# First attention of a decoder trunk: each head's product with V in its own half of the array's columns, one output bank, three transposition banks

## Chip, cores and metric

The kernel runs on one core of one Trainium2 chip. The metric is the device time of one execution in microseconds, the median of several runs. The engines are TensorE (PE; its weight loads are listed as PEld), VectorE (DVE), ScalarE (ACT), GpSimd (POOL) and SyncE (SP), which issues the DMAs. Each engine works through its own instructions in order and waits on semaphores of the others.

## The reference

The reference is one step of a two-layer decoder for a prompt of 1024 tokens and 64 sample tokens, width 1024. Layer one is a sparse attention with 16 heads of 64 and 2 KV heads; layer two is differential attention; each is followed by an MLP with a squared ReLU. The change touches only the prompt part of layer one. There each head has three branches, whose outputs are added with gates:

```
s = jnp.einsum('btkgd,bckd->bkgtc', qg, kc);  p_cmp = softmax(where(c_ok, s, NEG));  o_cmp = p_cmp @ vc
... the same over the selected blocks -> o_sel (with 16 blocks of 64 in all, every earlier block is selected)
... the same over the last 512 positions -> o_win
out = o_cmp * g[..., 0:1] + o_sel * g[..., 1:2] + o_win * g[..., 2:3]
```

## The kernel before

`nsa_prompt` works on 64 units, one for each pair of heads (p, 8 of them) and block of 128 query rows (i, taken in the order 0, 7, 1, 6, 2, 5, 3, 4). A unit has two halves.

`scores` does, for each head s of the pair, the score products on PE into PSUM tiles S (two tiles of two banks each), the row maxima on DVE (L692), the exponentials on ACT into an SBUF tile P (L695; six P tiles, so three units), a reciprocal on DVE (L699) and, on POOL, the scaling of P's three parts by gate and sum (L702). An S tile is free again when ACT has read it.

`values` takes the scaled P of both heads. It has nb = 3 to 14 blocks of 128 keys (branch 0 has one, branch 1 has i + 1, branch 2 up to five). PE transposes every block of P into a PSUM bank `tr`, two blocks of two heads to a bank (L110), and DVE or ACT, by turns, copies the bank to SBUF as PT (L99 or L97). There are two `tr` banks. Then the products with V follow, 64 columns of V as weights and PT as the moving operand, into a bank `av` (two of them). Before the change, one matmul has both heads side by side (256 columns), and the blocks go by turns to the upper and the lower 64 partitions of `av`, so that two matmuls, in the two halves of the array's columns, stand next to each other; with an odd number of blocks the last one is done head by head. The two halves are then added: ACT copies the first half to `oh` (L746), and DVE adds the second half to it, once for each head (L748), into the output tile oT.

All matmuls with V and all transpositions have f32 operands. A matmul with V is two records in the trace, a transposition one.

The generators `prep`, `scores` and `values` are interleaved by `stagger`: a tuple (start, length, steps, generator) spreads the steps over units of time, and a scheduler then puts the instructions into an order for each engine by when it expects operands and buffers to be there. The order is fixed when the program is built. The first matmuls of `values` are kept behind its last transposition (`issue_after`).

Of the kernel before, what the change touches and what calls it, by code (L numbers as in the profile page):

```python
# [12 lines left out]
AF = mybir.ActivationFunctionType  # L13
OP = mybir.AluOpType
AX = mybir.AxisListType
PSUM = bass.MemoryType.PSUM
# [46 lines left out]
def stagger(gens):  # L63

    order = [(t + (i + 0.5) * d / n, k) for k, (t, d, n, _) in enumerate(gens) for i in range(n)]
    for _, k in sorted(order):
        next(gens[k][3], None)
    for g in gens:
        run(g[3])


class Step:
# [551 lines left out]
    def nsa_prompt(self, oT):  # L624
        nc, io = self.nc, self.io
        cmN, A, B, V = self.cmN, self.A, self.B, self.V
        with ExitStack() as ctx:

            qp = self.pool(ctx, bufs=2, side="right")
            sp = self.pool(ctx)  # L630
            Sp, trp, avp = (self.pool(ctx, bufs=2, space=PSUM) for _ in range(3))
            st = {}

            def prep(p):
                k = p // 4
                X = [(sp if p % 2 else qp)("X", [128, NP], F32R, bufs=2) for _ in range(2)]
                st[p] = X
                qn = qp("qn", [128, 8, 128])
                nc.sync.dma_start(qn, self.zq[0:NP, p * 128:p * 128 + 128].rearrange("(t p) c -> p t c", p=128))
                for g in range(2):  # L640
                    cs = slice(g * 512, g * 512 + 512)
                    ps = trp("tr", [128, 512]) if p else Sp("S", [128, 1024])[:, 0:512]
                    for i in range(4):
                        self.tr(ps[:, i * 128:i * 128 + 128], qn[:, 4 * g + i, :], 128)
                    for s in range(2):
                        self.qk_prep(ps, s * 64, X[s][k * 64:k * 64 + 64, cs], X[s][64 - k * 64:128 - k * 64, cs])
                        yield
# [59 lines left out]
            def scores(p, i):  # L707
                for s in range(2):
                    yield from score(p, i, s)

            def values(p, i):


                k = p // 4
                ks = slice(k * 64, k * 64 + 64)
                P, w1, j0 = zip(*(st[p, i, s] for s in range(2)))
                w1, j0 = w1[0], j0[0]

                blocks = [(0, V[0][:, ks])]
                blocks += [(64 + j * 128, V[1][:, j, ks]) for j in range(i + 1)]  # L720
                blocks += [(64 + w1 + (j - j0) * 128, V[2][:, j, ks]) for j in range(j0, i + 1)]
                nb = len(blocks)
                PT = sp("PT", [128, 14, 2, 128], bufs=2)
                for x0, x1 in [(max(x, 0), x + 2) for x in range(-(nb % 2), nb, 2)]:
                    ps = trp("tr", [128, 2, 2, 128])
                    for x in range(x0, x1):
                        for s in range(2):
                            o = blocks[x][0]
                            last = self.tr(ps[:, x - x0, s], P[s][:, o:o + 128], 128)
                    self.n_p += 1  # L730
                    self.hi("va"[self.n_p % 2], PT[:, x0:x1], ps[:, 0:x1 - x0])
                    yield
                av = avp("av", [128, 256])
                todo = [(x, None) for x in range(nb - 1, nb % 2 - 1, -1)] + [(0, s) for s in range(2) if nb % 2]
                with self.tc.issue_after(last.ins):
                    for c, (x, s) in enumerate(todo):
                        h = slice(c % 2 * 64, c % 2 * 64 + 64)
                        y = PT[:, x] if s is None else PT[:, x, s]
                        if s is None:
                            o, y = av[h], y.rearrange("p a b -> p (a b)")  # L740
                        else:
                            o = av[h, s * 128:s * 128 + 128]
                        self.mm(o, blocks[x][1], y, c < 2, c >= len(todo) - 2)
                yield
                oh = sp("oh", [64, 256], bufs=2)
                nc.scalar.activation(oh, av[0:64], AF.Copy)  # L746
                for s in range(2):
                    nc.vector.tensor_tensor(oT[p][s * 64:s * 64 + 64, i * 128:i * 128 + 128],  # L748
                                            av[64:128, s * 128:s * 128 + 128], oh[:, s * 128:s * 128 + 128], OP.add)

            units = [(p, i) for p in range(8) for i in (0, 7, 1, 6, 2, 5, 3, 4)]
            gens = [(-1, 1, 4, prep(0))] + [(8 * p + 0.5, 7, 4, prep(p + 1)) for p in range(7)]
            for u, (p, i) in enumerate(units):
                ng = (i + 1 + min(i + 1, 5) + 2) // 2
                gens.append((u, 1, 4 if i < 3 else 8, scores(p, i)))
                gens.append((u + 1.2, 1, ng + 1, values(p, i)))
            stagger(gens)


# [811 lines left out]
```

## Time and profile before

| what | value |
|---|---|
| median of 3 runs | 3484.68 us (3480.68 to 3485.0) |
| the profiled execution | 3483.36 us |
| its span, first to last instruction | 3481.6 us (1.76 us lie around it) |
| first attention (first to last product with V) | about 480 to 995 us |
| PE busy over the span | 3351.3 us (96%) |
| DVE, ACT, POOL busy over the span | 1930.0, 1224.7, 749.1 us |

Busy time is the time in which an engine has an instruction recorded. The recorded end of a matmul is modelled, so a PE that is shown as busy may still stand still for a moment. A wait is idle time of an engine and is put down to the instruction that released it.

### The profile page before, as it was taken

The page shows a single profiled execution, that of the slowest core. Times are in us where ns is not written, and L with a number is a line of the kernel's source. Part 1 is how long each engine was busy: PE and PEld are TensorE (multiplying, and loading weights), DVE is VectorE, ACT ScalarE, POOL GpSimd, SP SyncE. Part 2 cuts the span into 40 slices and gives each one's busy share as a digit, 9 for nine tenths or more (in the row PEclk, how much of TensorE's full clock was granted, in tenths as well). Part 3 has the DMA queues.
Part 4 walks back from the last instruction along what each step waited for, and adds up shares of the span by engine and source line. Part 5 has one row for each costly group of instructions (what it writes and reads, how often), then busy time and mean ns, then how long its engine had stood idle before and what let it go on. Part 6 is the DMA issues. An engine that isn't in the chain of part 4 may idle for free.

```text
span 3481.6 us, 57136 instructions
## 1 busy us (share of the span) xinstructions
PE 3351.3 (96%) x21902; PEld 2821.0 (81%) x21902; DVE 1930.0 (55%) x4110; ACT 1224.7 (35%) x2976; POOL 749.1 (22%) x1036
## 2 busy tenths in 40 slices
PE   8989889999999999999999998999989999999998
PEld 7879666666679999999998876677769999999998
DVE  5355666666665544454447213777775444444445
ACT  5122466666653111111114121677763211111111
POOL 1242234444420001110004203222230100011102
PEclk9999999999999999999999999999999999999999
DMA  7333410000022111111113223666632111111111
GB/s 249 123 115 96 139 41 7 7 13 1 1 70 73 39 41 49 49 48 44 37 43 132 93 76 98 205 219 224 200 101 65 57 43 37 43 49 49 45 36 52
DMA packets 238283, 270.87 MB, mean 78 GB/s; under 512 B 19802, under 2 KB 186874, under 8 KB 237946
## 3 DMA queue, kind: packets, MB, share of 16 engines
q1 hardware_dynamic: 238010, 267.23, 24.2%
q8 instruction: 172, 2.82, 0.3%
q14 instruction: 101, 0.83, 0.1%
HBM read 229.81 MB, written 41.50 MB: 78 GB/s over the span
## 4 chain that ended last, share of the span: by engine, by line
PE 82%; DVE 6%; ACT 4%; SPq 2%; DMA 2%; issue 2%; POOL 1%; DVEq 0%; ACTq 0%; POOLq 0%
PE dn L107 26%; PE up L107 22%; PE ps L107 11%; PE S L107 6%; PE av L107 6%; PE tr L110 6%; PE hid L107 2%; ACT P L695 2%; SPq L143 2%; PE tr L107 1%; DVE ml L692 1%; POOL P L702 1%; DMA out_dram<-in_state_nsa_win_dram 1%; DVE PT L99 1%; DMA kv<-in_cache_nsa_sel_dram 0%
## 5 line engine op out<-in xcount | busy, mean ns | idle before, releaser
L1078 DVE TENSOR_TENSOR xT<-xT,dn 128x512 f32<-128x512 f32 (+2 forms) x768 | 404.3, 530 | 497.2 <-PE dn L107 496.3
L107 PE MATMUL dn<-xh,dh 128*128 128x512 f32 (+2 forms) x1536 | 504.5, 328 | 0.7 <-DVE xT L1078 0.7
L107 PE MATMUL up<-hh,uh 128*128 128x512 f32 (+2 forms) x1536 | 503.9, 328 | 1.2 <-DVE u L1054 1.2
L107 PE MATMUL dn<-xl,dh 128*128 128x512 f32 (+2 forms) x1536 | 504.6, 329 | 0.0
L107 PE MATMUL dn<-xh,dl 128*128 128x512 f32 (+2 forms) x1536 | 503.4, 328 | 0.0
L107 PE MATMUL up<-hh,ul 128*128 128x512 f32 (+2 forms) x1536 | 502.8, 327 | 0.0
L107 PE MATMUL up<-hl,uh 128*128 128x512 f32 (+2 forms) x1536 | 502.4, 327 | 0.0
L100 POOL TENSOR_SCALAR xh<-u 128x512 fp32r<-128x512 f32 (+2 forms) x192 | 142.3, 741 | 1310.0 <-PE dn L107 858.6
L1055 ACT ACTIVATE u<-u 128x512 f32<-128x512 f32 (+2 forms) x192 | 96.5, 503 | 829.0 <-DVE u L1054 827.0
L107 PEld LDWEIGHTS up<-hh,uh 128*128 128x128 f32 x1536 | 289.7, 189 | 25.1 <-DVE u L1054 1.8
L107 PEld LDWEIGHTS up<-hl,uh 128*128 128x128 f32 x1536 | 289.7, 189 | 22.3
L107 PEld LDWEIGHTS up<-hh,ul 128*128 128x128 f32 x1536 | 289.6, 189 | 22.2
L107 PEld LDWEIGHTS dn<-xh,dh 128*128 128x128 f32 x1536 | 289.5, 189 | 21.6 <-DVE xT L1078 1.3
L107 PEld LDWEIGHTS dn<-xh,dl 128*128 128x128 f32 x1536 | 289.2, 188 | 21.6
L107 PEld LDWEIGHTS dn<-xl,dh 128*128 128x128 f32 x1536 | 289.4, 188 | 19.9
L702 POOL TENSOR_SCALAR P<-P,ml,gates 128x64 f32<-128x64 f32 (+8 forms) x384 | 244.4, 652 | 282.2 <-DVE ml L699 255.2
L107 PE MATMUL ps<-wh,hh 128*128 128x512 f32 (+2 forms) x720 | 277.3, 386 | 7.1 <-ACT st L370 3.4
L107 PE MATMUL S<-A,X 128*128 128x512 f32 (+7 forms) x608 | 250.3, 412 | 29.1 <-ACT P L695 22.5
L107 PE MATMUL ps<-wh,hl 128*128 128x512 f32 (+1 forms) x720 | 277.6, 386 | 0.7 <-DVE hl L104 0.4
L107 PE MATMUL ps<-wl,hh 128*128 128x512 f32 (+2 forms) x720 | 276.8, 385 | 0.1
L110 PE MATMUL tr<-ident,P 128*128 128x128 f32 (+1 forms) x1584 | 245.0, 281 | 19.8 <-DVE PT L99 6.8
L695 ACT ACTIVATE P<-S,ml 128x64 f32<-128x64 f32 (+8 forms) x384 | 216.3, 571 | 86.0 <-DVE ml L692 65.1
(324 smaller groups left out, 6355.9 us busy)
## 6 DMA issues: line engine op xcount, KB each, us to landing
ur<-in_mlp_w_up_dram SPq DMA_DIRECT2D x64, 512.0 KB
dr<-in_mlp_w_down_dram SPq DMA_DIRECT2D x64, 512.0 KB
kt<-in_cache_diff_kv_dram SPq DMA_DIRECT2D x64, 512.0 KB
vt<-in_cache_diff_kv_dram SPq DMA_DIRECT2D x64, 512.0 KB
xT<-x_saved SPq DMA_DIRECT2D x16, 544.0 KB
zq<-ro SPq DMA_DIRECT2D x32, 256.0 KB
nat<-in_cache_nsa_cmp_dram SPq DMA_DIRECT2D x128, 64.0 KB
kv<-in_cache_nsa_sel_dram SPq DMA_DIRECT2D x64, 128.0 KB
```

What stands on the lines that cost most here:

```text
L99: return self.nc.vector.tensor_copy(out, x)
L100: return self.nc.gpsimd.tensor_scalar(out, x, 1.0, 0.0, op0=OP.mult, op1=OP.add)
L107: self.nc.tensor.matmul(out, lhsT, rhs, start=start, stop=stop)
L110: return self.nc.tensor.transpose(out, x, self.ident[:n, :n])
L143: self.page_dmas.append(self.nc.sync.dma_start(out, in_))
L692: nc.vector.tensor_reduce(nm[:, br:br + 1], x, AX.X, OP.max, negate=True)
L695: nc.scalar.activation(P[:, c:c + x.shape[1]], x, AF.Exp, bias=nm[:, br:br + 1], accum_out=l[:, br:br + 1])
L702: nc.gpsimd.tensor_scalar(P[:, c0:c1], P[:, c0:c1], l[:, br:br + 1], g[:, br:br + 1], op0=OP.mult, op1=OP.mult)
L1055: nc.scalar.activation(u[:, :w], u[:, :w], AF.Square)
L1078: nc.vector.tensor_tensor(x, x, ps[:, :w], OP.add)
```

## The change

The product with V is done for each block and each head as a matmul of 128 columns of its own, head 0 in the first 64 columns of the array and head 1 in the last 64, with the same slice of V as weights for both. `av` then holds head 0 in its upper 64 partitions and head 1 in its lower 64, as oT wants them. One DVE copy replaces ACT's copy and DVE's two additions. There is one `av` bank in place of two and three `tr` banks in place of two. `values` has one step more (ng + 2), spread over 1.2 units in place of 1. The loop over the transpositions is only written in another way.

```diff
-            Sp, trp, avp = (self.pool(ctx, bufs=2, space=PSUM) for _ in range(3))
+            Sp, trp, avp = (self.pool(ctx, bufs=n, space=PSUM) for n in (2, 3, 1))
...
-                av = avp("av", [128, 256])
-                todo = [(x, None) for x in range(nb - 1, nb % 2 - 1, -1)] + [(0, s) for s in range(2) if nb % 2]
+                av = avp("av", [128, 128])
                 with self.tc.issue_after(last.ins):
-                    for c, (x, s) in enumerate(todo):
-                        h = slice(c % 2 * 64, c % 2 * 64 + 64)
-                        y = PT[:, x] if s is None else PT[:, x, s]
-                        if s is None:
-                            o, y = av[h], y.rearrange("p a b -> p (a b)")
-                        else:
-                            o = av[h, s * 128:s * 128 + 128]
-                        self.mm(o, blocks[x][1], y, c < 2, c >= len(todo) - 2)
+                    for x in range(nb - 1, -1, -1):
+                        for s in range(2):
+                            self.mm(av[s * 64:s * 64 + 64], blocks[x][1], PT[:, x, s], x == nb - 1, x == 0)
                 yield
-                oh = sp("oh", [64, 256], bufs=2)
-                nc.scalar.activation(oh, av[0:64], AF.Copy)
-                for s in range(2):
-                    nc.vector.tensor_tensor(oT[p][s * 64:s * 64 + 64, i * 128:i * 128 + 128],
-                                            av[64:128, s * 128:s * 128 + 128], oh[:, s * 128:s * 128 + 128], OP.add)
+                nc.vector.tensor_copy(oT[p][:, i * 128:i * 128 + 128], av)
+                yield
...
-                gens.append((u + 1.2, 1, ng + 1, values(p, i)))
+                gens.append((u + 1.2, 1.2, ng + 2, values(p, i)))
```

What follows shows how instructions moved. The orders of POOL and SP are the same before and after; those of PE, DVE and ACT differ almost only inside the first attention.

PE, pair 4, before: what stands behind the last score product of unit 7's second head (tile S_9683; its scaled scores are P_9667, those of the first head P_9610).

```order
L107 MATMUL S_9683<-cmN_5453,identb_69 128x64
L110 MATMUL tr_9604<-ident_65,P_9430 128x128
...
L107 MATMUL S_9708<-A11_5641,X_8926 128x320
...
L107 MATMUL av_9619<-PT_9548,V2_6173 64x256 x5
L107 MATMUL av_9619<-PT_9548,V1_5636 64x256 x5
L107 MATMUL av_9619<-PT_9548,vcp_2238 64x128 x2
...
L107 MATMUL S_9747<-A11_5641,X_8927 128x320
...
L107 MATMUL S_9791<-A11_5641,X_8926 128x512
...
L110 MATMUL tr_9720<-ident_65,P_9610 128x128
L110 MATMUL tr_9720<-ident_65,P_9667 128x128
```

PE, the same place after the change (tile S_9987, second head P_9971, first head P_9903).

```order
L107 MATMUL S_9987<-cmN_5453,identb_69 128x64
L107 MATMUL S_10014<-A11_5641,X_9154 128x320
...
L110 MATMUL tr_10027<-ident_65,P_9903 128x128
L110 MATMUL tr_10040<-ident_65,P_9903 128x128
L107 MATMUL av_10005<-PT_9949,V2_6173 64x128 x2
L107 MATMUL av_10005<-PT_9949,V1_5636 64x128 x2
L107 MATMUL av_10005<-PT_9949,vcp_2238 64x128 x2
L110 MATMUL tr_10046<-ident_65,P_9903 128x128
L107 MATMUL S_10054<-A11_5641,X_9155 128x320
...
L107 MATMUL S_10092<-A11_5641,X_9154 128x512
...
L110 MATMUL tr_10027<-ident_65,P_9971 128x128
```

The transpositions of the second head now stand nearer behind its scores: three score tiles, a product with V of 3 blocks and three transpositions lie between; before there lay three score tiles, a product with V of 11 blocks and 15 transpositions. The first head's transpositions fill a place in each of the three banks before the second head's begin. A product with V has its matmuls at 128 columns, two for each block.

DVE, the end of pair 3 and the start of pair 4, before: where the outputs (L748) stand among maxima (L692), copies of transpositions (L99) and reciprocals (L699).

```order
L104 TENSOR_TENSOR X_9651<-tr_9654,X_9651 64x512
L748 TENSOR_TENSOR oT_4906<-av_9619,oh_12581 64x128
L99 COPY PT_9645<-tr_9677 128x512
L748 TENSOR_TENSOR oT_4906<-av_9619,oh_12581 64x128
L692 TENSOR_REDUCE ml_9746<-S_9747 128x1 x3
```

DVE, the same place after.

```order
L104 TENSOR_TENSOR X_9955<-tr_9958,X_9955 64x512
L739 COPY oT_4906<-av_9912 128x128
L99 COPY PT_9949<-tr_9980 128x512
L692 TENSOR_REDUCE ml_9972<-S_9987 128x1 x2
L692 TENSOR_REDUCE ml_10013<-S_10014 128x1 x3
L739 COPY oT_4907<-av_10005 128x128
```

The output's place among DVE's instructions is the same; it is one instruction instead of two, and it waits for PE alone.

## Rows read from the trace of the kernel before

**Rows 1.** The page: busy time, share of the span, instructions.
```profile
PE 3351.3 (96%) x21902; PEld 2821.0 (81%) x21902; DVE 1930.0 (55%) x4110; ACT 1224.7 (35%) x2976; POOL 749.1 (22%) x1036
```

**Rows 2.** Busy time by stretch, first attention: us, PE, PEld, DVE, ACT, POOL, clock.
```profile
480.00:995.00 515.00, 482.14 (x3751) 342.73 (x3751) 348.11 (x814) 340.92 (x998) 241.97 (x378) 1.00 0.02 6
```

**Rows 3.** Waits, 480 to 1000 us: us in total, times, longest.
```profile
DVE oT L748 <- ACT oh L746: 58.3, 42, 2.9
...
PE S L107 <- ACT P L695: 21.2, 41, 1.0
...
ACT P L695 <- PE tr L110: 12.9, 7, 1.9
...
PE tr L110 <- DVE PT L99: 6.5, 10, 0.8
...
PEld tr L110 <- POOL P L702: 4.0, 14, 0.4
...
PE tr L110 <- ACT PT L97: 3.3, 7, 0.6
```

**Rows 4.** Groups by line, 480 to 1000 us: busy us, mean ns, idle before.
```profile
L110 PE MATMUL tr<-ident,P 128*128 128x128 f32 x1178 | 174.2, 278 | 9.9 <-DVE PT L99 6.5 <-ACT PT L97 3.3
...
L107 PE MATMUL av<-PT,V 128*64 128x256 f32 x1056 | 133.0, 386 | 1.5 <-DVE PT L99 1.4
...
L748 DVE TENSOR_TENSOR oT<-av,oh 64x128 f32<-64x128 f32 x128 | 37.6, 294 | 60.5 <-ACT oh L746 58.3
...
L746 ACT ACTIVATE oh<-av 64x256 f32<-64x256 f32 x64 | 24.1, 376 | 38.7 <-PE av L107 38.2
```

**Rows 5.** Timeline of PE, a product with V of 13 blocks: start, us, count.
```profile
706.39 2.81 PE L107 MATMUL av<-PT,V 128*64 128x256 f32 x24
709.03 0.39 PE L107 MATMUL av<-PT,vcp 128*64 128x128 f32 x4
...
709.14 0.28 PE L107 MATMUL av<-PT,vcp 128*64 128x128 f32 x2
```

**Rows 6.** Timeline of PE, sample attention, products of 64 columns in both halves.
```profile
387.30 0.69 PE L107 MATMUL av<-PT,kv 128*64 128x64 f32 x16
```

**Rows 7.** Weight loads of the products with V, 480 to 1000 us.
```profile
L107 PEld LDWEIGHTS av<-PT,V 128*64 128x64 f32 x1056 | 71.6, 136 | 40.1 <-issue 4.4 <-DVE PT L99 3.2 <-ACT P L695 1.3
```

**Rows 8.** DVE's groups in the second attention, 2200 to 2600 us: a copy of one PSUM tile.
```profile
L1283 DVE COPY oT<-av 128x128 f32<-128x128 f32 x64 | 18.2, 285 | 12.0 <-PE av L107 11.3
```

**Rows 9.** The chain of waits, 705 to 714 us: start, us, what.
```profile
709.53 0.39 ACT oh L746
...
713.52 0.55 PE tr L110 x3
```

**Rows 10.** Timeline of PE and DVE: waits in brackets.
```profile
719.79 0.50 PE L107 MATMUL S<-A,X 128*128 128x512 f32 x1 [0.73 <-ACT P L695]
...
725.68 0.60 DVE L748 TENSOR_TENSOR oT<-av,oh 64x128 f32<-64x128 f32 x2 [1.09 <-ACT oh L746]
...
728.80 0.50 PE L107 MATMUL S<-A,X 128*128 128x512 f32 x1 [0.47 <-ACT P L695]
```

**Rows 11.** Timeline, pair 4, unit 7, second head: last score product, POOL's scaling, later PE work.
```profile
738.16 0.21 PE L107 MATMUL S<-cmN,identb 128*128 128x64 bf16 x1
...
741.46 2.05 POOL L702 TENSOR_SCALAR P<-P,ml,gates 128x1024 f32<-128x1024 f32 x2
...
743.13 0.39 PE L107 MATMUL S<-A,X 128*128 128x320 f32 x1
...
743.93 0.47 PE L107 MATMUL S<-A,X 128*128 128x512 f32 x1
...
745.09 0.61 PE L110 MATMUL tr<-ident,P 128*128 128x128 f32 x4
```

**Rows 12.** Timeline, pair 4, unit 5, second head: last score product, POOL's last scaling.
```profile
767.71 0.23 PE L107 MATMUL S<-masks,identb 128*128 128x128 bf16 x1
...
773.24 0.88 POOL L702 TENSOR_SCALAR P<-P,ml,gates 128x640 f32<-128x640 f32 x1
```

More of the change, by code (lines that the diff above doesn't have):

```diff
@@ L723, in values @@
                 PT = sp("PT", [128, 14, 2, 128], bufs=2)
-                for x0, x1 in [(max(x, 0), x + 2) for x in range(-(nb % 2), nb, 2)]:
+                for x0 in range(-(nb % 2), nb, 2):
+                    xs = range(max(x0, 0), x0 + 2)
                     ps = trp("tr", [128, 2, 2, 128])
-                    for x in range(x0, x1):
+                    for x in xs:
                         for s in range(2):
                             o = blocks[x][0]
-                            last = self.tr(ps[:, x - x0, s], P[s][:, o:o + 128], 128)
+                            last = self.tr(ps[:, x - xs[0], s], P[s][:, o:o + 128], 128)
@@ L730, in values @@
                     self.n_p += 1
-                    self.hi("va"[self.n_p % 2], PT[:, x0:x1], ps[:, 0:x1 - x0])
+                    self.hi("va"[self.n_p % 2], PT[:, xs[0]:x0 + 2], ps[:, 0:len(xs)])
                     yield
-                av = avp("av", [128, 256])
-                todo = [(x, None) for x in range(nb - 1, nb % 2 - 1, -1)] + [(0, s) for s in range(2) if nb % 2]
+                av = avp("av", [128, 128])
                 with self.tc.issue_after(last.ins):
-                    for c, (x, s) in enumerate(todo):
-                        h = slice(c % 2 * 64, c % 2 * 64 + 64)
-                        y = PT[:, x] if s is None else PT[:, x, s]
-                        if s is None:
-                            o, y = av[h], y.rearrange("p a b -> p (a b)")
-                        else:
-                            o = av[h, s * 128:s * 128 + 128]
-                        self.mm(o, blocks[x][1], y, c < 2, c >= len(todo) - 2)
```

## The prediction

> **What bounds the kernel now.** Over the whole span PE is busy 96% of the time [rows 1], so I asked first whether that holds in the stage that changes. [...] PE is the bound, and what DVE and ACT save is worth only what it takes from PE's 33 us of idle time. The list of waits names what ends that idle time: 21.2 us until ACT has read a score tile (41 times), 6.5 and 3.3 us until DVE or ACT has emptied a transposition bank (17 times) [rows 3], and 1.5 us before products with V [rows 4]. Each such wait is a little longer than shown, since a transposition is recorded with 0.28 us [rows 4] while four follow each other at (0.61 - 0.28)/3 = 0.11 us [rows 11]; 0.17 us of each wait is hidden behind that modelled end. So about 60 waits cost 32.4 + 60 x 0.17 = 43 us. That is the most the change can bring.
>
> **PE's own work: nothing.** A matmul with V is two passes. Before the change 24 records of 256 columns take from 706.39 to 709.03; they run two by two, one in each half of the columns, so a pair of passes takes 2.64/12 = 0.22 us [rows 5]. The block that is already done head by head gives the new form: its two passes of 128 columns begin at 709.03 and 709.14, 0.11 us apart, two records each [rows 5]. The 8 pairs of heads have 8 x 74 = 592 blocks. Before: 272 pairs of 256 columns and 48 of 128, 272 x 2 x 0.22 + 48 x 2 x 0.11 = 130 us; after: 592 x 2 x 0.11 = 130 us. The number of matmuls goes from 640 to 1184, and so does that of weight loads, which need cover. In the sample attention pairs of passes of 64 columns stand even nearer: 16 records, 8 pairs, in 0.69 us, the end of the last included [rows 6], under 0.09 us a pair with new weights in both halves each time. So loads for both halves fit within less than 0.11 us.
>
> [...]
>
> **Removed from ACT and DVE.** ACT loses 64 copies, 24.1 us; DVE loses 128 additions, 37.6 us [rows 4], and gets 64 copies of a 128x128 PSUM tile, 0.285 us each by the same form in the second attention [rows 8], 18.2 us. None of it lies on PE's path by itself. What matters is the order of the queue: DVE stood idle 58.3 us, 42 times, because an addition waited for ACT's copy [rows 3], and everything behind it, maxima and copies of transpositions, waited too.
>
> **PE's waits, one by one.**
> The transposition banks: 9.8 us visible and 17 x 0.17 hidden, 12.7 us. The chain shows a typical one: ACT copies at 709.53, DVE adds twice, and only then come the bank's copies, which let PE go on at 713.52 [rows 9]. The third bank gives a whole bank of slack, and the copy-out is one step shorter (ACT's 0.38 us and an addition of 0.29 fall away). But runs over three banks now stand in the order. I take 10 of 12.7. With it goes 1 of the 1.5 us before products with V.
> The P tiles: ACT waited 12.9 us, 7 times, for transpositions still reading an old P [rows 3], and PE stood 0.73 us each time because ACT's reading of the score tile came late [rows 10]. In the new order the transpositions stand nearer to their scores, so P is free earlier. 7 x (0.73 + 0.17) = 6 us, all of which I take.
> The addition in front of the maxima: at 725.68 DVE begins an addition after 1.09 us of idling for ACT, and the maxima behind it release PE at 728.80 after 0.47 us [rows 10]. Once for each pair, 8 x (0.47 + 0.17) = 5 us; I take 3. The other score waits stay: they are the length of score, maximum and exponential with two tiles.
>
> **Added: transpositions nearer to their scores.** In pair 4 the second head of unit 7 has its last score product at 738.16, and POOL's scaling is done at 741.46 + 2.05 = 743.51, 5.35 us later [rows 11]. By the new order PE has between them two score tiles like that from 743.13 to 743.93, 0.80 us each, one like that from 743.93 to 745.09, 1.16 us [rows 11], three transpositions, 0.33, and 3 blocks with V, 3 x 2 x 0.11 = 0.66, with about 0.2 for going over to them and back (from 709.14 to the next transposition it is 0.1 more than a pass): 3.9 us. It is 1.4 us short. The second head of unit 5 took from 767.71 to 773.24 + 0.88 = 774.12, 6.4 us [rows 12], and the order, counted the same way, leaves 4.7: 1.7 short. The other heads are short by 0.3 us at most. So PE could newly wait for POOL: 8 x (1.4 + 1.7) = 25 us if POOL's P comes as late as now, nothing if the score tiles in between wait for ACT anyway, which takes the same time. Today such waits are 4.0 us in 14 [rows 3]. I take 8, nearer to the lower end, because DVE and ACT in that chain lose their waits.
>
> **One output bank: nothing.** The next product with V waits for DVE's copy. At the nearest place, the end of a pair, four transpositions (0.44), two score tiles (some 1.0 and 0.80) and two transpositions lie between, 2.4 us; the copy needs 0.3 and stands behind at most one other copy in DVE's queue. Behind it, if PE did wait, all PE work would be queued.
>
> **Sum.** -10 - 1 - 6 - 3 + 8 = -12 us, against the profiled execution's own 3483.4: 3471 us. The execution lies 1.3 us under the median of the runs shown. A measurement of this kernel can tell 0.2%, 7 us, from no change.
>
> **Rivals.**
> More goes than I count (15%): the score waits shrink as a whole, since DVE gets 19 us back and ACT 24 us of 515, and no wait for POOL appears. Up to 43 us go: 3441 to 3460, say 3450. For it speaks that DVE's blocked 58 us stand ahead of most maxima; against it, that most score waits have no addition before them.
> The waits move (20%): what the banks give, the score tiles take back, as PE comes to the next tile earlier and ACT no earlier. Only some 4 us stay: 3480. For it speaks that 21 of 32 us of idling end at ACT, against it that ACT's own queue gets shorter.
> Slower, by the wait for POOL (10%): the 25 us come in full, and the gain at the score tiles is lost in it, since time that PE waits at a score tile is only moved to the transposition. 25 - 11 = +14: 3497. It decides from 8 x 1.4 us on, when the gain at the banks is eaten.
> Weight loads show (5%): if a pair of passes had to wait for its load's record, 0.136 us [rows 7] in place of 0.11, 592 x 2 x 0.026 = 31 us: 3471 + 31 = 3502. [Rows 5] and [rows 6] speak against it.
> The one output bank holds PE up (3%): half the units waiting 0.3 us, 10 us: 3481.
>
> **How the numbers follow.** The forecast, 3460 to 3478, has 47%. Faster by over 0.2%: the forecast and the first rival, 62%. Within 0.2%: the moved waits and the bank, 23%. Slower: POOL and the loads, 15%. The range of 8 in 10 runs from 3447, where most of PE's idling is gone, to 3492, half-way into the POOL case; it leaves out a part of the first rival and most of the slower ones.
>
> **What would show it.** Right: waits of transpositions for DVE or ACT under 4 us together; no wait of ACT for transpositions; DVE's outputs 18 us; spacing of the product's passes 0.11 us; PE idle around 20 us between 480 and 985. Wrong: PE or its loads waiting for POOL's P over 15 us; passes 0.13 us or more apart; a product with V waiting for DVE's output; or score waits grown by what the banks gave.

## The result, and the profile after

The changed kernel takes 3451.85 us (median of 6 runs, 3450.66 to 3458.3), the kernel before 3483.1 us (6 runs, 3479.97 to 3485.65) beside it: 0.9915 of the time, 95% interval 0.9905 to 0.9926, or 31 us less. The forecast was 3471. Among the six runs of the changed kernel the longer ones have the lower granted clock, as a mean over the execution (3458.3 us at 0.986, 3450.66 at 0.989).

The profiled execution of the changed kernel takes 3451.07 us with a span of 3449.3. Its page, the line that answers to [rows 1]:

```profile
PE 3345.2 (97%) x22990; PEld 2869.2 (83%) x22990; DVE 1911.0 (55%) x4046; ACT 1200.9 (35%) x2912; POOL 749.0 (22%) x1036
```

The table by stretch over the stage that changed, which is now shorter, for [rows 2] (columns as there):

```profile
480.00:965.00 485.00, 473.60 (x4824) 387.25 (x4824) 327.30 (x748) 317.23 (x937) 241.66 (x377) 1.00 0.03 7
```

PE's idle time is 485.0 - 473.6 = 11.4 us, where it was 515.0 - 482.1 = 33 [rows 2]. The list of waits from 480 to 970 us, for [rows 3]:

```profile
DVE oT L739 <- PE av L107: 36.7, 36, 2.7
...
PE S L107 <- ACT P L695: 9.0, 33, 0.9
...
PEld av L107 <- DVE PT L99: 1.2, 2, 1.0
...
PE av L107 <- DVE PT L99: 0.8, 1, 0.8
...
PE tr L110 <- ACT PT L97: 0.6, 1, 0.6
```

Transpositions wait for their banks once in place of 17 times; score tiles wait 9.0 us in place of 21.2; ACT's 12.9 us of waiting for transpositions and the loads' 4.0 us for POOL have no row any more. The groups by line over the same stretch, for [rows 4], [rows 7] and [rows 8]:

```profile
L110 PE MATMUL tr<-ident,P 128*128 128x128 f32 x1178 | 170.0, 277 | 0.7 <-ACT PT L97 0.6
...
L107 PE MATMUL av<-PT,V 128*64 128x128 f32 x2104 | 129.0, 276 | 0.8 <-DVE PT L99 0.8
...
L107 PEld LDWEIGHTS av<-PT,V 128*64 128x64 f32 x2104 | 113.5, 137 | 7.9 <-issue 2.4 <-DVE PT L99 1.2 <-DVE ml L692 1.2
...
L739 DVE COPY oT<-av 128x128 f32<-128x128 f32 x63 | 18.1, 287 | 38.2 <-PE av L107 36.7
```

PE's timeline at a product of 13 blocks, for [rows 5]: 48 records are 24 pairs of passes, one in each half of the columns, in 692.21 - 689.54 = 2.67 us, 0.11 us a pair.

```profile
689.54 2.84 PE L107 MATMUL av<-PT,V 128*64 128x128 f32 x48
692.21 0.39 PE L107 MATMUL av<-PT,vcp 128*64 128x128 f32 x4
```

**Where the 32.3 us between the two profiled executions lie.** From the first product with V to the last it takes 486.8 us (477.5 to 964.3) where it took 514.6 (480.7 to 995.3): 27.8 us. Another 1.2 us lie behind the stage (from there to the end 2485.1 us, before 2486.3). The remaining 3.2 us lie ahead of it, where the code is the same, and say nothing: in the profiles of this study the stage starts anywhere between 476.1 and 486.0 us.

**A finer measure.** The stage's first pair of heads also varies (last section), the seven others hardly do. So kernels are compared below by the time from the last product of the first pair to that of the last pair, "seven pairs". It stands in the row of the matmuls with `vcp`, the last block of every product, as first and last start. Kernel before:

```profile
L107 PE MATMUL av<-PT,vcp x200: 272/273/379, 547.4 to 995.3; 128*64 128x128 f32 x86, 128*64 128x256 f32 x14
```

Changed kernel:

```profile
L107 PE MATMUL av<-PT,vcp x228: 272/273/273, 539.8 to 964.3; 128*64 128x128 f32 x114
```

447.9 us became 424.5: 23.4 us less, 3.34 for each pair, 26.7 for eight if the first pair gained as much as the others.

### The profile page after: what moved, and what is told of

It is laid out like the page before. It is cut to its first block, busy times and chain, and to the rows that moved or that the text cites. A ratio compares the mean times of both kernels' runs of the same rounds, so it can differ in the third digit from the quotient of the medians.

```text
span 3449.3 us, 59178 instructions
## 1 busy us (share of the span) xinstructions
PE 3345.2 (97%) x22990; PEld 2869.2 (83%) x22990; DVE 1911.0 (55%) x4046; ACT 1200.9 (35%) x2912; POOL 749.0 (22%) x1036
## 4 chain that ended last, share of the span: by engine, by line
PE 66%; DVE 3%; ACT 1%; issue 0%; SPq 0%; DMA 0%; POOL 0%; DVEq 0%; ACTq 0%; POOLq 0%
PE dn L107 26%; PE up L107 22%; PE ps L107 8%; PE tr L110 3%; PE av L107 3%; PE S L107 2%; PE tr L107 1%; DVE hl L260 0%; DVE xT L1069 0%; DVE P L1252 0%; ACT oh L97 0%; DVE oT L104 0%; DVE ml L1234 0%; ACT P L1235 0%; DVE ur L1103 0%
```

## Experiments

All in one table; each was timed beside the kernel before on the same chip. Score waits are PE's for ACT at score tiles, bank waits those of transpositions for DVE or ACT (us, times in brackets, from 480 to 965 or 970 us, for the kernel before to 1000). In e2_form and e8_one_out the stage goes on to 987 and 994 us; over all of it their bank waits are 7.3 (11) and 6.0 (9), their score waits as listed.

| kernel | median us | ratio to before, 95% interval | seven pairs us | score waits | bank waits |
|---|---|---|---|---|---|
| before | 3483.1 | 1 | 447.9 | 21.2 (41) | 9.8 (17) |
| changed | 3451.85 | 0.9915, 0.9905 to 0.9926 | 424.5 | 9.0 (33) | 0.6 (1) |
| after_again, unchanged | 3451.84 | 0.9910, 0.9894 to 0.9927 | 424.5 | 8.4 (32) | 0.6 (1) |
| e1_banks | 3468.31 | 0.9958, 0.9942 to 0.9975 | 432.3 | 17.6 (31) | 1.7 (8) |
| e2_form | 3476.19 | 0.9982, 0.9973 to 0.9992 | 443.3 | 20.1 (39) | 6.5 (9) |
| e8_one_out | 3475.21 | 0.9969, 0.9958 to 0.9981 | 441.6 | 20.5 (40) | 5.5 (7) |
| e5_p5 | 3452.15 | 0.9913, 0.9896 to 0.9929 | 424.4 | 7.7 (31) | 0.6 (1) |
| e7_act_out | 3450.89 | 0.9902, 0.9886 to 0.9919 | 424.8 | 9.7 (33) | 0.6 (1) |
| e9_banks_dve | 3471.68 | 0.9955, 0.9939 to 0.9972 | 437.0 | 16.3 (25) | 1.7 (7) |
| e10_two_copies | 3455.01 | 0.9910, 0.9894 to 0.9927 | 426.3 | 10.5 (32) | 0.6 (1) |
| e11_handoff | 3458.48 | 0.9919, 0.9902 to 0.9935 | 424.5 | 10.7 (32) | 0.6 (1) |
| e4_reversed | 3458.69 | 0.9932, 0.9915 to 0.9948 | 426.9 | 5.8 (28) | 0.9 (2) |
| e12_shared | 3459.72 | 0.9934, 0.9918 to 0.9951 | 432.8 | 18.1 (40) | none |
| e13_load | 3458.74 | 0.9922, 0.9906 to 0.9939 | 428.0 | 12.3 (32) | 0.8 (2) |

The chips differ from run to run (the kernel before took 3482.2 to 3486.4 us on them), and kernels with the same seven pairs, 424.4 to 424.8 us, have medians from 3450.89 to 3458.48. So where the two disagree (e11_handoff), the seven pairs are the measure of the stage.

**e1_banks: the third transposition bank, taken from the output, and nothing else**, on the kernel before.

```diff
-            Sp, trp, avp = (self.pool(ctx, bufs=2, space=PSUM) for _ in range(3))
+            Sp, trp, avp = (self.pool(ctx, bufs=n, space=PSUM) for n in (2, 3, 1))
```

> The kernel before, with the banks of the change (two score tiles, three transposition banks, one output bank) and nothing else: the product with V, ACT's copy and DVE's two additions stay as they were. Its order of instructions has the transpositions as near to their scores as the changed kernel has (5.57 us of PE work at the lower quartile against 5.57 there and 7.58 before). Theory 'banks': the third bank and the order that comes with it give most; PE's waits for copies of transpositions fall under 2 us, ACT no longer waits for an old P, score waits fall by 7 or more of 21 us, and the time is 3462 to 3468 us. Rival 'copy-out': the shorter copy-out gives most; then this kernel gains 10 us at most (3473 or more), and could lose some where the single output bank is held until both additions are done.

Its waits of PE:

```profile
PE S L107 <- ACT P L695: 17.6, 31, 1.1
PE tr L110 <- DVE PT L99: 1.7, 8, 0.4
PE av L107 <- DVE PT L99: 0.7, 1, 0.7
```

447.9 - 432.3 = 15.6 us of the 23.4, two thirds, come with this one line. Not only bank waits go: score waits fall too, though by 3.6 us and not by the 7 expected, and ACT waits for a transposition once (1.7 us) in place of 7 times. Counted in the built orders of instructions, it is this line, and not the products' form, that moves the transpositions nearer to their scores. The line changes the room and, through the scheduler, the order; a third bank with the old order was not tried, so which of the two does it stays open.

**e2_form: everything but the banks**, on the changed kernel.

```diff
-            Sp, trp, avp = (self.pool(ctx, bufs=n, space=PSUM) for n in (2, 3, 1))
+            Sp, trp, avp = (self.pool(ctx, bufs=n, space=PSUM) for n in (2, 2, 2))
```

> The changed kernel with the banks of before (two score tiles, two transposition banks, two output banks): each head in its own half of the columns and one DVE copy, nothing else. In its order the transpositions stand as far from their scores as before (7.53 us at the lower quartile). Theory 'banks': 3472 to 3478 us, PE still waits 6 us or more for copies of transpositions and ACT still 10 us or more for an old P. Rival 'copy-out': 3455 to 3462 us, most of the gain is here.

```profile
PE S L107 <- ACT P L695: 20.1, 39, 0.9
PE tr L110 <- DVE PT L99: 6.5, 9, 0.8
```

4.6 us. New form and shorter copy-out without the third bank leave the score waits nearly as they were. A kernel with the old numbers in `stagger` needed no run: its order of instructions is that of the changed kernel on every engine, so that edit does nothing.

**e8_one_out: as e2_form, with one output bank.**

```diff
-            Sp, trp, avp = (self.pool(ctx, bufs=n, space=PSUM) for n in (2, 3, 1))
+            Sp, trp, avp = (self.pool(ctx, bufs=n, space=PSUM) for n in (2, 2, 1))
```

> The changed kernel with two transposition banks and one output bank, a bank less than the run with two and two. If one output bank holds PE up nowhere, the time is that of that run, 3473 to 3479 us, and no product with V waits for DVE's copy. If it costs, 3480 us or more, with waits of the product for the copy of 5 us or more.

441.6 us, 1.7 less than with two output banks, and no product waits for the copy of the one before. All of the 1.7 us lies in the last pair; the six pairs before it take 386.2 us here and 386.3 in e2_form (391.1 before the change). One output bank costs nothing.

**e5_p5: five P tiles in place of six**, on the changed kernel; the order of instructions is the same.

```diff
-                P = sp("P", [128, 64 + 1024 + 640], bufs=6)
+                P = sp("P", [128, 64 + 1024 + 640], bufs=5)
```

> The changed kernel with five P tiles in place of six, the order of instructions on each engine unchanged. By the order an old P is then read last 0.35 us of PE work after the new scores are done (it was 4.93 us before them with six), as in the kernel before. If the early release of P is worth what the prediction took (6 us), this kernel takes 3456 to 3462 us, ACT waits for transpositions 8 us or more again and the score waits grow by 5 or more. If P's release never mattered, it stays at 3450 to 3454.

The one new row in its waits:

```profile
ACT P L695 <- PE tr L110: 0.6, 1, 0.6
```

Seven pairs take 424.4 us: in the changed kernel even the sixth tile is spare.

**e7_act_out: the output copied by ACT**, on the changed kernel.

```diff
-                nc.vector.tensor_copy(oT[p][:, i * 128:i * 128 + 128], av)
+                nc.scalar.activation(oT[p][:, i * 128:i * 128 + 128], av, AF.Copy)
```

> The changed kernel with the one copy-out on ACT in place of DVE. If the gain of the copy-out is only that there are fewer steps between the product and the freed queues, the engine is of no matter: 3449 to 3455 us. If it matters that DVE waits for PE ahead of the maxima, ACT does better (3447 or less). If ACT is the engine that PE waits for (all of the 9.0 us of score waits end at ACT), ACT's waiting for the product holds the exponentials: 3458 us or more.

Seven pairs take 424.8 us: the engine of the one copy does not matter.

**e9_banks_dve: the third bank, and DVE in place of ACT for the first copy**, on the kernel before.

```diff
-            Sp, trp, avp = (self.pool(ctx, bufs=2, space=PSUM) for _ in range(3))
+            Sp, trp, avp = (self.pool(ctx, bufs=n, space=PSUM) for n in (2, 3, 1))
...
-                nc.scalar.activation(oh, av[0:64], AF.Copy)
+                nc.vector.tensor_copy(oh, av[0:64])
```

> The kernel with the banks alone (3468 us), where DVE and not ACT copies the first half of the output: the two additions no longer wait for ACT, and DVE has some 0.3 us a unit more to do. Theory 'handoff' (DVE held until ACT has copied keeps the maxima, and so the score tiles, late): 3454 to 3461 us, score waits from 17.6 down to 12 or less. Rival 'work' (what counts is the time that DVE and ACT spend on the output): 3466 us or more.

437.0 us. In two stretches of this profile the granted clock is below 1.00, as the table by stretch shows (the clock is the third number from the end):

```profile
610.00:620.00 10.00, 8.57 (x57) 6.53 (x55) 8.08 (x22) 4.67 (x19) 4.83 (x8) 0.84 0.01 2
...
870.00:880.00 10.00, 10.00 (x75) 7.85 (x75) 6.62 (x13) 7.89 (x21) 5.39 (x11) 0.86 0.00 1
```

By an estimate that takes the work there to be as much slower as the clock is lower (last section), they can account for 10 x 0.16 = 1.6 and 10 x 0.14 = 1.4 us. The 434.0 us left are no better than the 432.3 of e1_banks. DVE also has 26.5 us of copies more to do (0.415 us each); priced as in e10_two_copies that is some 2.7 us, an estimate, and would leave a gain of 1 us. So what the banks alone lack is not DVE's standing by for ACT's copy.

**e10_two_copies: the output copied by DVE in two halves**, on the changed kernel; DVE works some 18 us longer in the stage.

```diff
-                nc.vector.tensor_copy(oT[p][:, i * 128:i * 128 + 128], av)
+                for s in range(2):
+                    nc.vector.tensor_copy(oT[p][s * 64:s * 64 + 64, i * 128:i * 128 + 128], av[s * 64:s * 64 + 64])
```

> The changed kernel with the copy-out as two DVE copies of 64 partitions each, 0.29 us more of DVE for a unit, 18 us in all, with no new wait for another engine. Theory 'handoff': 3451 to 3455 us. Rival 'work': 3457 us or more, the score waits up by 4 us or more.

Its group of copies:

```profile
L740 DVE COPY oT<-av 64x128 f32<-64x128 f32 x128 | 36.5, 285 | 38.5 <-PE av L107 36.7
```

Twice the work costs 1.8 us over seven pairs, a tenth of what DVE works longer.

**e11_handoff: ACT copies the bank to SBUF, DVE that to oT**, on the changed kernel.

```diff
-                nc.vector.tensor_copy(oT[p][:, i * 128:i * 128 + 128], av)
+                oh = sp("oh", [128, 128], bufs=2)
+                nc.scalar.activation(oh, av, AF.Copy)
+                nc.vector.tensor_copy(oT[p][:, i * 128:i * 128 + 128], oh)
```

> The changed kernel with the handoff of before put back: ACT copies the output of both heads to SBUF, and DVE copies from there to its place. The matmuls, the banks and the order of the transpositions are those of the changed kernel. Theory 'handoff': DVE waits 40 us or more for ACT's copy again, score waits 15 us or more, 3462 us or more. Rival 'work': DVE's copy from SBUF is no longer than that from PSUM, ACT has 18 us more, so 3453 to 3458 us.

Its waits have DVE standing idle for ACT again, and its `vcp` row gives 424.5 us:

```profile
DVE oT L741 <- ACT oh L740: 43.5, 34, 2.4
```

```profile
L107 PE MATMUL av<-PT,vcp x228: 272/273/273, 546.4 to 970.9; 128*64 128x128 f32 x114
```

43.5 us of blocked DVE cost PE nothing here. With three transposition banks the theory that this standing by is what the changed kernel got rid of falls. With two it can be worth no more than the 4.6 us of e2_form, products' form included.

**e4_reversed: POOL's three scalings in reverse order**, on the changed kernel.

```diff
-                for br, c0, c1 in ((0, 0, 64), (1, 64, 64 + w1), (2, 64 + w1, 64 + w1 + w2)):
+                for br, c0, c1 in ((2, 64 + w1, 64 + w1 + w2), (1, 64, 64 + w1), (0, 0, 64)):
```

> The changed kernel with POOL's three scalings of a head in reverse order (the same work): the block that the first transposition of a head reads is now scaled last, so every head's first transposition waits for all three scalings, as the prediction had counted it. If the prediction's price for the POOL wait was too high only because the first transpositions needed the second scaling and not the third, waits of transpositions or their loads for POOL now appear, 8 to 25 us in 480 to 970 us, and the time is 3460 to 3475 us. Rival: the score tiles that lie between wait for ACT at the same time and cover POOL whole; then waits for POOL stay under 2 us and the time stays at 3450 to 3457 us (the scheduler moves some products, with about 2 us more of changes between kinds of matmul).

Its waits:

```profile
PEld tr L110 <- POOL P L702: 1.0, 2, 0.6
...
PE tr L110 <- POOL P L702: 0.6, 2, 0.4
```

Under 2 us of waits, as the rival had it, but the run does not put the question that it was built for. In the order that the scheduler made for it, the block that is scaled last goes back to the third to fifth place of its head in 33 of 128 heads, among them the second head of unit 7 in all eight pairs; there the first transposition reads columns that the second scaling has finished, as in the changed kernel. So the scheduler went round the wait, and whether score tiles would have covered it is not shown: here they wait 5.8 us and not 9.0. Seven pairs take 2.4 us more. The median is 6.9 us above that of after_again, timed beside it, but the two intervals overlap; what of that is real beyond the 2.4 us stays open.

**e12_shared: four banks shared by transpositions and output**, on the changed kernel, an attempt to go further.

```diff
-            Sp, trp, avp = (self.pool(ctx, bufs=n, space=PSUM) for n in (2, 3, 1))
+            Sp, trp = (self.pool(ctx, bufs=n, space=PSUM) for n in (2, 4))
...
-                av = avp("av", [128, 128])
+                av = trp("tr", [128, 128])
```

> The changed kernel with one pool of four PSUM banks that transpositions and output share, in place of three and one. In the changed kernel the output bank stands empty most of the time, and the trace shows 1.4 us of PE waiting for a transposition's copy, with hidden parts under 2 us more. If transposition banks still held PE up, the stage goes from 486.8 to some 484 us and the time to 3448 us. Rival: the banks have given all they have, what is left is the score tiles' waiting for ACT (9 us in 33): no change, within 2 us.

Its waits of PE:

```profile
PE S L107 <- ACT P L695: 18.1, 40, 0.9
PE tr L107 <- DVE PT L99: 1.0, 1, 1.0
```

Both expectations miss: bank waits are gone altogether, yet seven pairs take 8.3 us more, and the score waits have doubled. With a fourth bank to fill, the scheduler puts transpositions into fewer and longer runs (168 runs in the stage's order on PE, 216 in the changed kernel). That the longer runs cause the waits was not tried apart from this, and their number alone does not decide: e1_banks has 202 runs, the kernel before 214, and e1_banks is faster.

**after_again: the changed kernel once more.**

> The changed kernel unchanged, beside the other two on the same chip. Stage from first to last product with V 486 to 488 us, as in its first profile, and 3449 to 3456 us, if the stage's length is what repeats and the start of the stage is what scatters.

Its `vcp` row:

```profile
L107 PE MATMUL av<-PT,vcp x228: 272/273/273, 544.6 to 969.1; 128*64 128x128 f32 x114
```

424.5 us again. The whole stage takes 489.1 us, 2.3 more than in the first profile and 1.1 above the expected band; all of it is in the first pair.

**e13_load: the copy-out in three instructions again**, on the changed kernel.

```diff
-                nc.vector.tensor_copy(oT[p][:, i * 128:i * 128 + 128], av)
+                oh = sp("oh", [128, 128], bufs=2)
+                nc.scalar.activation(oh, av, AF.Copy)
+                for s in range(2):
+                    h = slice(s * 64, s * 64 + 64)
+                    nc.vector.tensor_tensor(oT[p][h, i * 128:i * 128 + 128], av[h], oh[h], OP.max)
```

> The changed kernel with the copy-out made as long again as before: ACT copies the output bank to SBUF, and DVE puts the bank and the copy together in two instructions of 64 partitions (the maximum of two equal values, in place of the addition). PE's order stays nearly that of the changed kernel. From the last product of the first pair to that of the last it takes 424.5 us in the changed kernel, 426.3 with two DVE copies, 424.5 with one step by ACT ahead, and 432.3 with the banks alone. If what the banks alone lack is the load and the length of the copy-out together, these seven pairs take 430 to 433 us and the time is 3457 to 3461 us. Rival: it is the products' form and the order that goes with it on PE; then they take 424.5 to 427 us, and the time is 3450 to 3456 us.

```profile
L107 PE MATMUL av<-PT,vcp x228: 272/273/273, 541.3 to 969.3; 128*64 128x128 f32 x114
```

428.0 us, between the two: neither theory alone. The copy-out, with length and load together, is worth 428.0 - 424.5 = 3.5 us. The other 432.3 - 428.0 = 4.3 us between this kernel and e1_banks go with the products' form, the order that it gives on PE, and ACT's part of the copy-out, which is lighter here than there (64 copies of 0.277 us in place of 0.376); which of these, no run tells.

So the 23.4 us of seven pairs are, taken in this order, 15.6 for the banks with the order that comes with them, 3.5 for the shorter copy-out and 4.3 for the rest. The parts hang together: without the third bank, form and copy-out bring only 4.6, or 6.3 with one output bank, in place of 7.8.

## Why the prediction was right in direction and short in size

The time is in the range and on the forecast side. But the forecast's own range, 3460 to 3478, was missed: what happened is the first rival, to which 15% was given (the score waits shrink as a whole, no wait for POOL appears, 3441 to 3460). Its number came true, its reason in the main did not: it spoke of the time that DVE and ACT get back, but 18 us of DVE's are worth 1.8 us (e10_two_copies), and two thirds of the gain come with the banks.

**PE's own work: nothing. Right.** The pairs of passes stand 0.11 us apart with loads of their own, as in [rows 5] (in [rows 6], with 64 columns, under 0.09); the loads' records, 0.137 us each, lie beside other work: PEld is busy for 387.25 us and PE for 473.60 of the same 485.0.

**The transposition banks, -10 and -1. Right.** Bank waits fell from 9.8 to 0.6 us, and 16 waits at 0.17 us hidden go with them: 9.2 + 2.7 = 11.9; products waiting for PT fell from 1.5 to 0.8. That is 12.6 us against 11.

**The score waits, -6 and -3. Right in direction, too small, and for the wrong reasons.** They fell from 21.2 to 9.0 us, with 8 times fewer 0.17 hidden: 13.6 us against 9. The sentence "the other score waits stay" failed: of the 13.6, e1_banks shows 3.6 + 10 x 0.17 = 5.3 with the banks alone. And the two waits that the prediction did price had other causes. ACT's waits for an old P went as forecast, with the banks, but were worth little. Timeline of DVE and ACT in the kernel before, at the wait behind which PE stood 0.73 us in [rows 10]:

```profile
716.25 0.60 DVE L748 TENSOR_TENSOR oT<-av,oh 64x128 f32<-64x128 f32 x2 [1.53 <-ACT oh L746]
...
717.49 0.95 DVE L692 TENSOR_REDUCE ml<-S 128x1 f32<-128x64 f32 x2
...
718.55 0.32 ACT L695 ACTIVATE P<-S,ml 128x64 f32<-128x64 f32 x1 [1.86 <-PE tr L110]
```

ACT's start at 718.55 is put down to a transposition, but DVE's maximum, which ACT needs as well, had ended only at 717.49 + 0.95 = 718.44. Had P been free earlier, ACT would have gained a tenth of a microsecond there. e2_form bears this out. There PE has the same order around this place, ACT waits last for DVE and not for an old P, and DVE no longer waits for ACT:

```profile
712.04 0.32 ACT L695 ACTIVATE P<-S,ml 128x64 f32<-128x64 f32 x1 [1.79 <-DVE ml L692]
...
713.27 0.50 PE L107 MATMUL S<-A,X 128*128 128x512 f32 x1 [0.64 <-ACT P L695]
...
718.72 0.29 DVE L739 COPY oT<-av 128x128 f32<-128x128 f32 x1 [0.83 <-PE av L107]
...
722.30 0.50 PE L107 MATMUL S<-A,X 128*128 128x512 f32 x1 [0.47 <-ACT P L695]
```

PE still waits 0.64 us where it waited 0.73: the P tiles were worth some 0.1 us a time, under 1 us in all, where 6 were taken. It still waits 0.47 us where it waited 0.47 behind the additions of [rows 10], so those were worth nothing there, where 3 were taken. That e13_load gives 3.5 us for the whole copy-out does not make up for it, since that is not the wait that was priced. All five waits that PE has at score tiles in a pair stand at the same tiles in e2_form as before, with the same length within 0.1 us (0.30 to 0.90 before, 0.36 to 0.90 there). They go with the third bank and the order that it brings: e1_banks has four in a pair, of 0.33 to 0.83 us, at other tiles, the changed kernel four of 0.16 to 0.28. So that the two terms point the right way is luck.

**Transpositions nearer to their scores, +8. Wrong: 0.** This is the step that failed most. Pair 4, unit 7, second head, POOL and PE after the change, against [rows 11]:

```profile
728.47 2.05 POOL L702 TENSOR_SCALAR P<-P,ml,gates 128x1024 f32<-128x1024 f32 x2
...
729.65 2.31 POOL L702 TENSOR_SCALAR P<-P,ml,gates 128x640 f32<-128x640 f32 x4
```

```profile
725.22 0.21 PE L107 MATMUL S<-cmN,identb 128*128 128x64 bf16 x1
...
727.75 0.41 PE L107 MATMUL S<-A,X 128*128 128x320 f32 x1 [0.20 <-ACT P L695]
...
728.95 0.51 PE L107 MATMUL S<-A,X 128*128 128x512 f32 x1 [0.19 <-ACT P L695]
...
730.13 1.15 PE L110 MATMUL tr<-ident,P 128*128 128x128 f32 x9
```

POOL is done at 728.47 + 2.05 = 730.52, 5.30 us behind the last score product: as late as the 5.35 that the prediction took. But PE reaches the transposition only 4.91 us behind it, not 3.9, since two of the three score tiles in between wait for ACT (the "nothing if" of that step), and it starts 0.39 us before POOL's end: it reads a part of P that the second scaling has finished, and the third scaling starts at 729.65, 4.43 us behind the last score product. The prediction's 1.4 us was counted to the third scaling; counted to the second it is 4.4 - 3.9 = 0.5 us, and the score tiles cover that here. How much they would cover if the first transposition did need the third scaling, e4_reversed does not tell. Time that PE spends at a score tile is not there to be spent again at the next transposition.

**One output bank: nothing. Right**, by e8_one_out and by the list of waits.

**The sum.** Measured by the waits: 12.6 + 13.6 = 26.2 us, against 26.7 by the seven pairs and 27.8 for the stage. Of the 14 us between this and the forecast's 12, the POOL wait is 8, the score waits 4.6, the banks 1.6. But the two causes that the 9 us for score waits were put down to account for under 1 us, so the step at the score waits was further off than its sum. PE's idle time, forecast at about 20 us, is 11.4.

## What to carry to other kernels

Where one engine is the bound and its order is fixed when the program is built, price a PSUM bank by a run and not by the waits listed for it: moved to where tiles queue it gave more here, and the order around the waits behind it changed with it. That can also go the other way: four banks in a shared pool lost 8 us again. Before a new wait is priced, count to the instruction that is really waited for, and take off what the engine already waits for on the way. Before a listed wait is priced, look at when its other operands came, and at a run in which its supposed cause is gone.

## What the runs showed of the hardware

Around the start of the stage the granted clock falls for a while from 1.00 to 0.50, at a place that differs between executions of one kernel. By stretches of 0.5 us it is 0.50 from 471.5 to 477.5 us in the profile of the kernel before and from 470.0 to 476.0 in the first one of the changed kernel; the other stretches from 464 to 480 us have 1.00, but for one at each edge (0.52 to 0.66). In the latter profile score products of 128x512 begin 0.43 us apart at 0.50 (471.06 and 471.49) and 0.23 at 1.00 (476.85 and 477.08). So a mean between the two levels over a longer stretch is read here as a part of it at 0.50. The table by stretch of after_again (columns as in [rows 2]):

```profile
450.00:460.00 10.00, 9.06 (x99) 6.07 (x98) 7.14 (x17) 5.88 (x18) 2.88 (x4) 1.00 0.25 67
460.00:470.00 10.00, 7.41 (x97) 5.78 (x97) 4.31 (x14) 4.78 (x20) 1.25 (x1) 0.83 0.08 19
470.00:480.00 10.00, 8.82 (x44) 6.83 (x45) 6.12 (x23) 5.50 (x23) 2.48 (x6) 0.66 0.13 37
480.00:490.00 10.00, 8.44 (x51) 6.14 (x51) 6.54 (x17) 6.32 (x24) 6.32 (x9) 0.74 0.01 2
```

PE was busy for 9.06 of 10 us in the last stretch at 1.00, and for 7.41 in the one in which it first falls. In the first profile of the same kernel the clock was back at 1.00 from 480 us on, and the first pair took 62.3 us (477.5 to 539.8); in this one 64.6 (480.0 to 544.6). Seven pairs behind it took 424.5 us in both. So a stage's steady part could be compared here to a few tenths of a microsecond, while the medians of kernels with the same steady part lie up to 7.6 us apart.
